# Sixteen sums of token pieces in the first layer: GpSimd in place of VectorE

## The chip, the cores and the metric

The kernel runs on one core of one Trainium2 chip. The metric is the device time of one execution in microseconds (us). The engines are TensorE (PE in the profile; PEld is its weight load), VectorE (DVE), ScalarE (ACT), GpSimd (POOL) and SyncE (SP), the last of which only issues DMAs here. Each engine works through its own queue in order; engines wait for one another by semaphores. GpSimd issues DMAs too, in the same queue as its own arithmetic.

## The reference, cut to what matters

Two layers, each on 512 tokens of 2048 features:

```
def hybrid_layer(x, ...):
    h = rmsnorm(x, g_pre)
    z = h @ w_in                 # the nine parts of z: two head groups and their gates
    ...                          # gated linear attention, chunked attention, SiLU gates
    y = jnp.concatenate([o_gla, o_att], axis=-1) @ w_out
    return x + rmsnorm(y, g_post)
```

All is float32. What matters here are the large products with `w_in` and the operand `h` that goes into them.

## The kernel before, in words

**Precision.** TensorE is fed in a rounded format (fp32r). Each operand is therefore split in two: a high part, which ScalarE makes by copying the value into the rounded format, and a low part, which VectorE makes by subtracting the high part from the value (`split`, lines 109 and 110, for tokens; `Job.high`, line 261, and `Job.low`, line 271, for weights). A product then is three matmuls: high by high, high by low, low by high.

**Products.** Most of the large products are done in pairs of blocks by the Strassen-Winograd scheme (`fast_gemm`): seven products P1 to P7, each over four chunks c of 512 features (two halves of 256), in place of eight. The token side is cut in four pieces: a11 and a12 from the first 256 tokens (feature halves 0 and 1, in `full[0, c][:, kh]`), a21 and a22 from the last 256 (`full[1, c][:, kh]`). P1, P2 and P4 take pieces as they are (a11, a12, a22). The others take sums of pieces: S1 = a21 - a22 for P5 (by the code's names), S2 = S1 - a11 for P6, S4 = a12 + S2 for P3, S3 = a11 - a21 for P7. With four chunks these are the sixteen sums of the title. They are made in place in the tiles of the pieces (128x512 float32) by `token_sums`: `make` picks the operands, `sub` does the sum, and `put` splits the result (high part on ScalarE, low part on VectorE) and stores the split in device memory for later block pairs by a DMA from GpSimd's queue.

**The weight side.** The raw weights come in by SP's DMAs, and VectorE makes the weight sums (lines 255 and 257). For the first pair of value blocks and for the pair of gate blocks ("parted" and "summed" in `Job`) the sum for P5 is made by the DMA itself: `Job.add` (lines 181 and 184) issues from GpSimd's queue a DMA that accumulates the second block onto the tile that held P1's weights. It has to wait until P1's high and low parts were read from that tile, and P5's high part waits until it has landed.

**The twin pairs of the first layer.** After the first gate block (`std_gemm`, lines 380 and following) the layer does the value pair (AV0, AV1: 512 columns) and the gate pair (AG1 with AG2: 264 columns) as twins: for each (k, c) of `PROD_TWIN` one step of the one and one step of the other, in the order P2, P1, P5, then P6 and P3 in turn, P7, P4. This takes about 50 to 168 us of the profile. In the same time `first_operands` (lines 783 and 799) still makes the pieces of the last 256 tokens, splits a22 and stores the split, and then `token_sums(0)` runs as a task: the first four sums (S1 of the four chunks) one after the other, and each later one only when the gate product that uses the sum of four places before has been written into the program, since the splits of S2, S4 and S3 share a ring of four buffers ("sa") with one another and with the splits of a22. The splits of S1 have homes of their own (`HOMES0`).

**What sets the order.** The program is laid out by a planner. It takes instructions by their place in the program and by when its own simulated clock has their data ready, for each engine. `tc.issue_after(x)` ties the instructions in its block that are on x's engine behind x on that engine; it says nothing to other engines. Before the change `sub` is tied on VectorE behind the low part made two jobs back (`lows[-2]`), and the high part in `put` behind the last weight cast on ScalarE (`last_cast[0]`). The second layer makes its sums elsewhere in its order and without such a tie.

The lines of the profile that matter: L473 matmuls of a fast product, L261 high part and L271 low part of a weight, L255 and L257 weight sums, L109 and L110 high and low part of tokens, L649 the token sums of both layers, L662 the store of a split token sum, L799 the store of the split a22, L181 and L184 the accumulating loads, L524 a small power on GpSimd in the norms of later parts.

Of the kernel before, what the change touches and what calls it, by code (L numbers as in the profile page):

```python
# [36 lines left out]
def hybrid_trunk(  # L37
# [14 lines left out]
    nc = tc.nc  # L52
# [20 lines left out]
    def slot(tag, shape, dtype=F32):  # L73
        return slots.tile([P] + shape, dtype, tag=tag, name=nm(tag))

    def rtile(tag, shape=(2, W), dtype=F32, bufs=4):
        return ring.tile([P] + list(shape), dtype, tag=tag, name=nm(tag), bufs=bufs)
# [27 lines left out]
    def flat(t):  # L105
        return t.bitcast(F32).rearrange("p a b -> p (a b)")

    def split(hi, lo, src):
        nc.scalar.copy(hi, src)  # L109
        return nc.vector.tensor_tensor(out=lo, in0=src, in1=hi.bitcast(F32), op=ALU.subtract).ins  # L110
# [39 lines left out]
    lows, loads, last_turn, first_high = [], [], [None], []  # L150
# [491 lines left out]

    def token_sums(l):
        tags, dst, home = ("g10", "g16", "H", "g0", "g1"), sa_d[l], HOMES if l else HOMES0
        stage, tied = [0], [False]

        def sub(out, a, b, op=ALU.subtract):
            with tc.issue_after(lows[-2]) if tied[0] else nullcontext():
                nc.vector.tensor_tensor(out=out, in0=a, in1=b, op=op)  # L649

        def put(name, c, src):
            if (name, c) in home:
                op = A[name, c] = slot(home[name, c], [2, 512], F32R)
            elif l == 0:
                op = A[name, c] = rtile("sa", (2, 512), F32R)
            else:
                tag = tags[stage[0] % len(tags)]
                op = rtile(tag, dtype=F32R) if tag == "H" else slot(tag, [2, 512], F32R)
                stage[0] += 1
            with tc.issue_after(last_cast[0]):  # L660
                split(op[:, 0, :], op[:, 1, :], src)
            nc.gpsimd.dma_start(dst[name, c], flat(op))  # L662
            written.add((id(dst), name, c))

        def make(name, c):
            a11, a12 = (full[0, c][:, kh, :] for kh in range(2))
            a21, a22 = (full[1, c][:, kh, :] for kh in range(2))
            if name == "S1":
                sub(a22, a21, a22)
                put(name, c, a22)  # L670
            elif name == "S2":
                sub(a22, a22, a11)
                put(name, c, a22)
            elif name == "S4":
                sub(a12, a12, a22, ALU.add)
                put(name, c, a12)
            else:
                sub(a21, a11, a21)
                put(name, c, a21)

        if l:
            for c in range(4):
                for name in ("S1", "S3", "S2", "S4"):
                    yield
                    make(name, c)
            yield
        else:
            names = [("S1", c) for c in range(4)] + [(n, c) for c in range(4) for n in ("S2", "S4")]
            names += [("S3", c) for c in range(4)]
            left = {v: k for k, v in LEFT.items()}  # L690
            for i, (name, c) in enumerate(names):
                tied[0] = True
                if i >= 4:
                    n, c0 = names[i - 4]
                    while (0, AG1, left[n], c0) not in issued:
                        yield
                make(name, c)
                yield
# [146 lines left out]
    def layer(l):  # L845
# [132 lines left out]
        if l:  # L978
            std_gemm(l, AG0, (0, 1), CO, operand_in, gate_evac(0), rate=1.3)
            roles.reverse()  # L980
            acc = {n: [ps_mm.tile([P, W], F32, tag="mm", name=nm("mm")) for _ in range(2)] for n in "YX"}
            fast_gemm(l, PAIRS[0], av_consume, rate=2.5, prod=PROD_FRONT, acc=acc)
            until(lambda: all((kh, 1, c) in A for kh in range(2) for c in range(4)))
            tasks.append(token_sums(l))
            std_gemm(l, AG0, (2, 3), CO, operand_in, gate_evac(0), rate=1.3)
            fast_gemm(l, PAIRS[0], av_consume, rate=1, prod=PROD_REST, acc=acc)
            drain()
            fast_gemm(l, GATE_PAIR, gate_consume, prod=PROD_GATE)
        else:
            std_gemm(l, AG0, range(NT), CO, operand_raw, raw_evac, rate=0.5, lag=1)  # L990
            acc = {n: [ps_mm.tile([P, W], F32, tag="mm", name=nm("mm")) for _ in range(2)] for n in "YX"}
            acc_g = {n: [aux()[:, :N1] for _ in range(2)] for n in "YX"}
            twins = [
                fast_gemm(l, pair, consume, rate=1, acc=z, steps=True)
                for pair, consume, z in ((PAIRS[0], av_consume, acc), (GATE_PAIR, gate_consume, acc_g))
            ]
            tasks.append(token_sums(l))
            for k, c in PROD_TWIN:
                if (k, c) == ("P5", 0):
                    acc["Z"] = [ps_mm.tile([P, W], F32, tag="mm", name=nm("mm")) for _ in range(2)]  # L1000
                for step in twins:
                    step(k, c)
            drain()
            roles.reverse()
# [664 lines left out]
```

## Time and profile before

| | |
|---|---|
| median of three runs | 1583.02 us (1580.74 to 1584.38) |
| the profiled execution | 1582.65 us, span of the instructions 1580.5 us |
| granted TensorE clock, mean | 0.999 |
| busy | PE 99%, DVE 81%, ACT 59%, POOL 9% of the span |
| token sums on VectorE (L649), both layers | 32 of about 0.68 us each |

How to read it. A busy time is a sum over the whole span; an engine that is busy 81% on the average can be full in one stretch and idle in another, so the stretch that the change touches has to be read by itself. A matmul's duration in the records overlaps the next one's, so the pace of TensorE is read from starts, not from durations. In a row of the timeline the first number is the start in us from the span's start, the second the duration, and a bracket at its end names how long the engine was idle before and what released it. In the chain of waits each row is a piece of the chain that ended last: start, length, and the engine and line that it went through.

### The profile page before, as it was taken

To read this page: it belongs to the slowest core of one execution; us is meant where nothing else is said; L and a number is where in the kernel's file an instruction comes from. 1 tells how busy PE (TensorE), PEld (TensorE's weight loads), DVE (VectorE), ACT (ScalarE), POOL (GpSimd) and SP (SyncE) were. 2 spreads that over 40 slices of the span, in tenths; PEclk is the share of its full clock that TensorE was granted. 3 is DMA by queue.
4 is the path that set the end of the run, shared out by engine and by line. 5 is a ranking of instruction groups with operands and counts; after the bars stand their busy time and mean duration, and the time that the engine had idled before them with its cause. 6 is when DMAs were issued, how large, how long until landed. Compare 5 with 4: busy or idle time off the path is not lost.

```text
span 1580.5 us, 24991 instructions
## 1 busy us (share of the span) xinstructions
PE 1570.5 (99%) x9054; PEld 1363.2 (86%) x9054; DVE 1287.6 (81%) x1723; ACT 928.6 (59%) x1551; POOL 138.9 (9%) x230
## 2 busy tenths in 40 slices
PE   9999999999999999999999999999999999999998
PEld 7888999998888777888888899999988887788886
DVE  5989968578786978998989878785886878699887
ACT  7655545657555556665786446455674655576644
POOL 0221000001000000100122000001010000001001
PEclk9999999999999999999999999999999999999999
DMA  9888895785859768689879998847969597686987
GB/s 370 264 263 295 306 332 190 229 304 183 312 173 313 271 227 306 241 301 387 304 250 360 368 332 312 307 148 235 332 213 313 175 334 263 233 297 226 343 302 206
DMA packets 137738, 439.40 MB, mean 278 GB/s; under 512 B 15364, under 2 KB 27908, under 8 KB 137584
## 3 DMA queue, kind: packets, MB, share of 16 engines
q1 hardware_dynamic: 118800, 372.65, 67.3%
q0 software_dynamic: 18528, 64.88, 12.1%
q8 instruction: 71, 1.16, 0.3%
q14 instruction: 51, 0.42, 0.1%
q10 hardware_dynamic: 288, 0.30, 0.1%
HBM read 378.20 MB, written 61.62 MB: 278 GB/s over the span
## 4 chain that ended last, share of the span: by engine, by line
PE 94%; DMA 3%; DVE 1%; ACT 1%; issue 0%; POOL 0%; SPq 0%; POOLq 0%; DVEq 0%; ACTq 0%
PE mm L473 54%; PE mm L463 20%; PE ax L473 6%; PE mm L380 4%; PE ax L1089 2%; PE ax L1071 1%; PE ax L1278 1%; PE ax L1248 1%; DMA g<-in_w_ag_dram 1%; DMA A<-sa 1%; PE ax L1051 1%; PE ax L1049 1%; PE ax L1050 1%; DVE wl L271 1%; DMA sa<-S 0%
## 5 line engine op out<-in xcount | busy, mean ns | idle before, releaser
L473 PE MATMUL mm<-wh,sa 128*128 128x512 f32 (+1 forms) x1600 | 502.6, 387 | 0.8 <-DMA sa<-S 0.8
L473 PEld LDWEIGHTS mm<-wh,sa 128*128 128x128 f32 x1600 | 296.9, 188 | 61.6 <-DMA sa<-S 1.2
L261 ACT CAST wh<-raw 128x1024 fp32r<-128x1024 f32 (+2 forms) x233 | 234.3, 1009 | 191.3 <-PE mm L473 69.5
L271 DVE TENSOR_TENSOR wl<-raw,wh 128x1024 fp32r<-128x1024 f32 (+2 forms) x233 | 269.5, 1162 | 75.9 <-PE mm L473 33.7
L261 ACT CAST wh<-H 128x1024 fp32r<-128x1024 f32 (+1 forms) x208 | 211.9, 1021 | 177.9 <-PE mm L473 62.3
L473 PE MATMUL mm<-wl,sa 128*128 128x512 f32 (+1 forms) x800 | 310.1, 388 | 0.4 <-DVE wl L271 0.4
L271 DVE TENSOR_TENSOR wl<-H,wh 128x1024 fp32r<-128x1024 f32 (+1 forms) x208 | 245.0, 1179 | 47.4 <-PE mm L473 18.3
L463 PE MATMUL mm<-sa,wh 128*128 128x256 f32 x1280 | 236.1, 284 | 0.0
L473 PE MATMUL mm<-wh,a 128*128 128x512 f32 (+1 forms) x672 | 215.4, 387 | 0.0
L463 PEld LDWEIGHTS mm<-sa,wh 128*128 128x128 f32 x1280 | 199.8, 191 | 0.5
L463 PE MATMUL mm<-sa,wl 128*128 128x256 f32 x640 | 180.6, 284 | 0.0
L473 PEld LDWEIGHTS mm<-wl,sa 128*128 128x128 f32 x800 | 150.2, 188 | 30.9 <-DVE wl L271 1.6
L473 PEld LDWEIGHTS mm<-wh,a 128*128 128x128 f32 x672 | 124.4, 188 | 24.2
L255 DVE TENSOR_TENSOR H<-H,raw 128x1024 f32<-128x1024 f32 (+1 forms) x120 | 141.0, 1180 | 0.3
L473 PE MATMUL mm<-wl,a 128*128 128x512 f32 (+1 forms) x336 | 130.8, 390 | 0.5 <-DVE wl L271 0.5
L261 ACT CAST wh<-g 128x1024 fp32r<-128x1024 f32 x84 | 81.3, 974 | 76.3 <-DVE g L255 25.7
L463 PEld LDWEIGHTS mm<-sa,wl 128*128 128x128 f32 x640 | 122.1, 191 | 0.2
L473 PE MATMUL mm<-wh,g 128*128 128x512 f32 (+1 forms) x416 | 120.5, 367 | 0.0
L271 DVE TENSOR_TENSOR wl<-g,wh 128x1024 fp32r<-128x1024 f32 x84 | 93.7, 1119 | 16.3 <-PE mm L463 7.4
L463 PE MATMUL mm<-a,wh 128*128 128x256 f32 x512 | 94.9, 285 | 0.0
L524 POOL TENSOR_TENSOR sm<-sm,mhalf 128x2 f32<-128x2 f32 (+2 forms) x40 | 38.9, 973 | 615.7 <-DVE sm L1099 295.7
L421 ACT COPY ev<-mm 128x512 f32<-128x512 f32 (+1 forms) x112 | 64.2, 573 | 45.8 <-PE mm L473 31.2
(284 smaller groups left out, 2493.7 us busy)
## 6 DMA issues: line engine op xcount, KB each, us to landing
raw<-in_w_dram SPq DMA_DIRECT2D x287, 512.0 KB, 5.4
sa<-S SPq DMA_DIRECT2D x176, 512.0 KB, 4.4
sa<-A SPq DMA_DIRECT2D x48, 512.0 KB, 6.0
H<-in_w_dram SPq DMA_DIRECT2D x48, 512.0 KB, 5.1
sa<-oS SPq DMA_DIRECT2D x32, 512.0 KB, 5.8
g<-in_w_dram SPq DMA_DIRECT2D x20, 512.0 KB, 7.0
S<-g POOLq DMA_DIRECT2D x18, 512.0 KB, 7.9
raw<-in_w_ag_dram SPq DMA_DIRECT2D x32, 264.0 KB, 4.5
```

Of the source, the lines that this page charges most:

```text
L255: nc.vector.tensor_tensor(out=h, in0=h, in1=r, op=ALU.add)
L261: last_cast[0] = nc.scalar.copy(self.wh[:, z, :], src[:, z, :]).ins
L271: last_low[0] = nc.vector.tensor_tensor(out=self.wl[:, z, :], in0=self.src[:, z, :], in1=self.wh[:, z, :].bitcast(F32), op=ALU.subtract).ins
L380: nc.tensor.matmul(pss[o], a(part, kk, o) if callable(a) else a[:, part, t], rhs[:, kk, :], start=(i == 0 and kk == 0 and m == 0), stop=(i ...
L421: last_copy[0] = nc.scalar.copy(e, src[t]).ins
L463: nc.tensor.matmul(dst, lhs[:, kk, f], a[:, part, tok], start=(fresh and kk == 0 and m == 0 and ft % 2 == 0), stop=(c == 3 and kk == 1 and ...
L473: last_mm[0] = nc.tensor.matmul(out_ps[t], a[:, part, tok], rhs[:, kk, :], start=(fresh and kk == 0 and m == 0), stop=(c == 3 and kk == 1 ...
L524: nc.gpsimd.tensor_tensor(out=out_r, in0=v, in1=mhalf[:, : v.shape[-1]], op=ALU.pow)
L1049: nc.tensor.matmul(ps[:, :n], self.qh[:, t], self.kh[:, :n], start=True, stop=False)
L1050: nc.tensor.matmul(ps[:, :n], self.qh[:, t], self.kl[:, :n], start=False, stop=False)
L1051: nc.tensor.matmul(ps[:, :n], self.ql[:, t], self.kh[:, :n], start=False, stop=True)
L1089: nc.tensor.matmul(o, self.pt[i][:, j * P : (j + 1) * P], av[hd // 4, j // 2][:, j % 2, (hd % 4) * P : (hd % 4 + 1) * P], start=(j == 0), ...
```

## The change

In the first layer the sixteen sums are issued on GpSimd in place of VectorE, and the tie behind the low part two jobs back goes. The operands, the results and the place in the program are the same, and so are `put` with its tie on ScalarE, the low parts on VectorE and the stores. The second layer's sums stay on VectorE; they had no tie before either, since `tied[0]` was set in the first layer's branch alone.

```
     def token_sums(l):
         tags, dst, home = ("g10", "g16", "H", "g0", "g1"), sa_d[l], HOMES if l else HOMES0
-        stage, tied = [0], [False]
+        stage = [0]
 
         def sub(out, a, b, op=ALU.subtract):
-            with tc.issue_after(lows[-2]) if tied[0] else nullcontext():
-                nc.vector.tensor_tensor(out=out, in0=a, in1=b, op=op)
+            (nc.vector if l else nc.gpsimd).tensor_tensor(out=out, in0=a, in1=b, op=op)
...
             for i, (name, c) in enumerate(names):
-                tied[0] = True
                 if i >= 4:
                     n, c0 = names[i - 4]
                     while (0, AG1, left[n], c0) not in issued:
```

More of the change, by code (lines that the diff above doesn't have):

```diff
@@ L644, in token_sums @@
         tags, dst, home = ("g10", "g16", "H", "g0", "g1"), sa_d[l], HOMES if l else HOMES0
-        stage, tied = [0], [False]
+        stage = [0]
         def sub(out, a, b, op=ALU.subtract):
-            with tc.issue_after(lows[-2]) if tied[0] else nullcontext():
-                nc.vector.tensor_tensor(out=out, in0=a, in1=b, op=op)
+            (nc.vector if l else nc.gpsimd).tensor_tensor(out=out, in0=a, in1=b, op=op)
         def put(name, c, src):
@@ L691, in token_sums @@
             for i, (name, c) in enumerate(names):
-                tied[0] = True
                 if i >= 4:
```

## The prediction, made before the result was known

> **What bounds the kernel now.** I read the page first, then the waits of TensorE over the whole span, then the stretch that holds the first layer's twin pairs (about 50 to 168 us) by windows, chain of waits and timeline.
>
> ```profile
> span 1580.5 us, 24991 instructions
> ...
> PE 1570.5 (99%) x9054; PEld 1363.2 (86%) x9054; DVE 1287.6 (81%) x1723; ACT 928.6 (59%) x1551; POOL 138.9 (9%) x230
> ...
> PE 94%; DMA 3%; DVE 1%; ACT 1%; issue 0%; POOL 0%; SPq 0%; POOLq 0%; DVEq 0%; ACTq 0%
> ```
> ```profile
> PE mm L473 <- DVE wl L271: 0.9, 2, 0.5
> PE mm L473 <- DMA sa<-S: 0.8, 1, 0.8
> ```
>
> TensorE (PE) is busy for 99% of the span and makes 94% of the chain that ended last. In the whole run its matmuls of the value and projection blocks waited 0.9 us for low parts from VectorE (DVE). So an edit that relieves DVE has little to win: it can only take away PE's waits, and those of the stretch in question are the next thing to price.
>
> The windows below are the stretch cut at its own turns: 66 to 82 holds the S1 sums, 82 to 101 the P5 pairs, 101 to 140 the P6/P3 and first P7 pairs. Columns: us, then busy time of PE, PEld, DVE, ACT, POOL, then clock, DMA share, GB/s.
>
> ```profile
> 66.00:82.00 16.00, 16.00 (x94) 14.18 (x93) 16.00 (x25) 10.98 (x18) 8.37 (x11) 1.00 1.02 250
> 82.00:101.00 19.00, 18.92 (x109) 16.56 (x108) 13.49 (x20) 8.28 (x13) 4.97 (x9) 1.00 0.99 302
> 101.00:140.00 39.00, 38.59 (x223) 33.81 (x222) 38.81 (x53) 24.49 (x39) 5.50 (x11) 1.00 0.70 237
> ```
>
> DVE has no idle time in 66 to 82, 5.51 us in 82 to 101 and 0.19 us in 101 to 140. PE lacks 0.08 and 0.41 us. DVE is full, but so is PE: a full DVE is here only just fast enough. Where PE did wait, its pace shows how much it lost:
>
> ```profile
> 96.96 0.39 PE L473 MATMUL mm<-wh,g 128*128 128x512 f32 x1
> ...
> 101.50 0.64 PE L473 MATMUL mm<-wh,sa 128*128 128x512 f32 x2
> ```
> ```profile
> 102.54 2.56 PE mm L473 x10
> 105.10 1.45 PE ax L473 x12
> 106.55 2.75 PE mm L473 x12
> 109.30 1.45 PE ax L473 x12
> 110.74 2.75 PE mm L473 x12
> ```
>
> A pair step (one value-block and one gate-block product) takes 110.74 - 106.55 = 4.19 us without a wait. The step from 96.96 to 101.50 took 4.54. The first P6 product, from 101.50, has its twelve value matmuls end at 105.10 by the chain, 3.60 after it began, where later ones have 2.75. The losses are so 0.35 and at most 0.85: the sums can win back at most about 1.2 us here. What made these losses is in the chain of the same stretch:
>
> ```profile
> 85.64 11.90 DMA g<-in_w_ag_dram
> 98.17 0.62 ACT sa L109
> 99.43 0.70 DVE wl L271
> 100.13 0.62 DVE g L255
> 100.75 0.60 DVE g L649
> 101.35 1.15 DVE wl L271
> ```
>
> The chain goes through GpSimd's (POOL's) DMA queue: the last accumulating load of a gate block (`add`, line 181), which lands at 97.54; then ScalarE's high part, and DVE's low part, a weight sum, one of the sixteen sums (L649, 0.60) and the low part that PE waits for.
>
> **The change part by part.** (1) Sixteen DVE sums go. One took:
>
> ```profile
> L649 DVE TENSOR_TENSOR g<-g x8: 674/680/693, 70.6 to 835.1; 128x512 f32<-128x512 f32 x8
> ```
>
> Back to back the next one starts 0.60 us later (100.75 + 0.60 = 101.35), so DVE is relieved of 16 x 0.60 = 9.6 us. Nearly all of it lies beside PE and is worth nothing; the one sum on the chain is worth 0.60.
>
> (2) Sixteen POOL subtractions or additions of 128x512 come. The trace has none; its nearest rows are fills:
>
> ```profile
> L753 POOL MEMSET t<- x1: 208/208/208, 13.4 to 13.4; 128x128 f32 x1
> L863 POOL MEMSET g<- x2: 277/277/277, 89.8 to 867.2; 128x192 f32 x2
> ```
>
> 64 columns more take 69 ns, so 512 columns are 277 + 320 x 1.08 = 623 ns for one pass. Two inputs and one output are one to three passes: 0.62 to 1.87 us. I take two passes, 1.24, since the write can run beside the reads. The Trainium skill (GPSIMD Engine Reference, "Elementwise — side-by-side cycle accounting") gives 4497 ns for 2048 columns; a quarter is an estimate of 1.12 us, and the sum would not move by it.
>
> (3) POOL's queue is in order, so each sum delays the DMAs behind it, and a sum waits behind a DMA that waits.
>
> ```profile
> 84.25 0.55 POOL L662 DMA_DIRECT2D S<-g  x1 [0.66 <-DMA A<-sa]
> 85.64 0.88 POOL L181 DMA_DIRECT2D g<-in_w_ag_dram  x1 [0.83 <-issue]
> ...
> 89.27 0.53 POOL L662 DMA_DIRECT2D S<-g  x1 [0.69 <-DMA S<-g]
> ```
>
> Here an issue waits for an earlier DMA to land ("<-DMA A<-sa", "<-DMA S<-g"): the queue is full, the add takes 11.90 us to land, and two issues are 1.39 us apart. So a late issue costs nothing while the queue has a backlog, and four sums (about 5 us) fit into the 7.63 us that POOL is not busy in 66 to 82. What costs is order: whatever is put ahead of the last add moves its landing by one place, about 1.3 us. The store of the fourth S1 (issued 89.27) can do so. Its sum waited on DVE until 81.50 although its input, the low part of A22, was done at 79.23:
>
> ```profile
> 78.55 0.68 DVE L110 TENSOR_TENSOR sa<-g,sa 128x512 fp32r<-128x512 f32 x1
> ...
> 81.50 0.68 DVE L649 TENSOR_TENSOR g<-g 128x512 f32<-128x512 f32 x1
> ```
>
> On POOL, without a tie, it can start at 79.3 and its split and store follow. Bounds 0 and +1.3 (+2.6, if a second store also goes ahead); I take +1.3, because that store was only 3.6 us behind the add.
>
> (4) The ties go. Instead of standing behind the low part two back, a sum can stand as soon as its data are there: the S3 sums after S1, S2 after the split of S1. So I expect many of the sums before 101, in the 5.51 us that DVE has idle, and the splits (their high parts still tied to the last cast on ScalarE) a little earlier. Nobody on DVE waits for them there.
>
> (5) Do POOL and DVE get in each other's way? This is the disputed cost. Rows of the small powers on POOL:
>
> ```profile
> 263.44 1.04 POOL L524 TENSOR_TENSOR sm<-sm,mhalf 128x4 f32<-128x4 f32 x1 [88.44 <-DVE sm L1099]
> ```
> ```profile
> 364.76 1.88 POOL L524 TENSOR_TENSOR sm<-sm,mhalf 128x4 f32<-128x4 f32 x1 [12.12 <-DVE sm L1099]
> ```
> ```profile
> 364.53 1.21 DVE L271 TENSOR_TENSOR wl<-H,wh 128x1024 fp32r<-128x1024 f32 x1
> ```
> ```profile
> 463.03 1.26 DVE L271 TENSOR_TENSOR wl<-H,wh 128x1024 fp32r<-128x1024 f32 x1
> ```
>
> The same power takes 1.04 us alone and 1.88 when DVE's two-input low part began 0.23 before it; it ended 0.90 after that low part (366.64 against 365.74). So POOL waited. The other way round the loss is small in the trace (a low part that began beside a power took 1.26 instead of 1.21), but that power reads four columns, not 512. Bounds for DVE's loss per sum: 0 and a whole POOL sum, 1.24 (1.87 at three passes). I take 0.6, about what DVE is relieved of, in the middle of 0 and 1.24: DVE is then neither freer nor fuller, and only the place counts. What a sum costs DVE in 66 to 82 delays PE by less than the roughly 1 us that PE would lose at 97 to 105 anyway while it waits for the last add; the two don't add.
>
> The sum: profiled execution 1582.65 (span 1580.5 and 2.15 around it); -0.60 for the sum that leaves the chain, +1.3 for the last add, 0 for DVE: 1583.35. The median of the three runs is 0.37 above the profiled one, so I forecast 1583.7 as a median. A measurement of this kernel can tell about 0.2%, 3.2 us: this is no change.
>
> **The rivals**, their times with the 0.37 as well. *A, relief only.* The store stays behind the add and POOL does not hold DVE up. Then all of 1.2 us comes back: 1581.8. For it: PE's waits there are DVE's low parts. Against it: the low parts waited for a DMA themselves. Still within 0.2%.
>
> *B, DVE becomes the bound (slower).* If a POOL sum keeps DVE from its two-input work for its whole length h, DVE's need grows. In the P6/P3 pairs:
>
> ```profile
> 104.23 1.22 DVE L271 TENSOR_TENSOR wl<-raw,wh 128x1024 fp32r<-128x1024 f32 x1
> ```
> ```profile
> 111.90 1.21 DVE L271 TENSOR_TENSOR wl<-raw,wh 128x1024 fp32r<-128x1024 f32 x1
> ```
>
> DVE turned two pairs round in 7.67 us with two sums among them, PE takes 2 x 4.19 = 8.38. With the sums on POOL DVE needs 7.67 - 1.20 + 2h, so it decides from h = 0.96. At h = 1.24 PE loses 0.57 in two pairs, at 1.5 1.09, at 1.87 1.83; the four such rounds (eight P6 and P3 pairs) make 2.3, 4.4 and 7.3 us. At 1.5: 1587.4, and 1590.3 at the end of it. For it: the power's 1.88, and DVE without idle time. Against it: sums that run before 101 aren't in these rounds, and then the rounds have 1.2 us to spare each. The Trainium skill (SBUF — State Buffer, "Who interferes with whom") says that a VectorE instruction with two inputs in SBUF and a GpSimd one that reads SBUF exclude each other, the second to issue waiting for the whole of the first; the trace agrees on POOL's side (1.88 against 1.04) and cannot show DVE's with 512 columns.
>
> *C, the queue.* Two stores and one POOL sum get ahead of the last adds while the queue runs dry: 2.6 + 1.2 - 0.6 = +3.2 at most, 1585 to 1586.2. For it: adds, stores and sums share one in-order queue; against it: the backlog.
>
> *D, something far away.* The planner lays out all later work anew, and waits of the other layers go (the 0.8 for sa<-S, the low parts). To be faster by 3.2 us nearly all of PE's waits would have to vanish: 1579.8.
>
> **How the numbers follow.** Forecast 0.47, A 0.17, B 0.24, C 0.08, D 0.04. The forecast's own range is 1582 to 1585.5. With A, C and the lower half of B, 1581.0 to 1587.5 holds a little over eight in ten. B counts as slower from 1586.2 (3.2 over the median), so from h = 1.4, which I hold for most of it, and with a little of C; D alone is faster: 0.04 faster, 0.72 no change, 0.24 slower.
>
> **What would show it.** Right: the sums stand on POOL at 1.0 to 1.9 us each, most before 101; DVE has more idle time in 82 to 101 or the same; the chain still goes over the last add, which lands at 98 to 99; PE's pairs keep 4.19. B: PE's matmuls wait for low parts several times in 66 to 140, low parts take over 1.5 us beside POOL sums. A: no wait at 97 to 105. Wrong altogether: a gain or loss outside 50 to 170 that is greater than inside.

## The result, and the profile after

| | before | after |
|---|---|---|
| median of six runs | 1582.08 us (1580.74 to 1584.38) | 1593.94 us (1592.46 to 1597.31) |
| profiled execution | 1582.65 us | 1593.94 us |
| granted TensorE clock, mean | 0.999 | 0.997 |

The changed kernel takes 1.0069 times as long (95% interval 1.0059 to 1.008): some 11 us slower, where the prediction said no change and a range up to 1587.5. It fell outside on the slow side.

The page of the changed kernel, for the lines shown of before: span, busy times, and the chain's shares by engine.

```profile
span 1591.4 us, 25003 instructions
...
PE 1575.6 (99%) x9054; PEld 1365.1 (86%) x9054; DVE 1298.9 (82%) x1707; ACT 928.4 (58%) x1551; POOL 168.8 (11%) x246
...
PE 95%; DMA 1%; DVE 1%; ACT 1%; issue 1%; POOL 1%; SPq 0%; POOLq 0%; DVEq 0%; ACTq 0%
```

VectorE has sixteen instructions fewer and is busy 11.3 us longer (1298.9 against 1287.6). That is the result in one line: what was taken off it came back, and as much again. The page alone doesn't say where; a share of 99% for PE looks the same in both.

The same three windows as before (us, then busy time of PE, PEld, DVE, ACT, POOL, clock, DMA share, GB/s):

```profile
66.00:82.00 16.00, 11.34 (x65) 9.30 (x64) 16.00 (x14) 8.98 (x16) 13.39 (x11) 0.96 0.97 226
82.00:101.00 19.00, 17.98 (x81) 14.74 (x82) 19.00 (x16) 5.62 (x9) 16.35 (x17) 0.85 0.90 231
101.00:140.00 39.00, 38.27 (x217) 33.17 (x216) 35.44 (x38) 22.27 (x35) 16.35 (x15) 1.00 0.61 214
```

Read the counts, not the busy times. In 66 to 82 VectorE was full before and is full now, but with 14 instructions instead of 25 (four of the 25 were sums); in 82 to 101 with 16 instead of 20, and its 5.51 idle us are gone. PE did 65 matmuls for 94 and 81 for 109. A full engine that does less work is being held up inside its instructions. The timeline of VectorE shows them:

```profile
77.53 4.17 DVE L271 TENSOR_TENSOR wl<-g,wh 128x1024 fp32r<-128x1024 f32 x1
...
82.84 2.44 DVE L110 TENSOR_TENSOR sa<-g,sa 128x512 fp32r<-128x512 f32 x1
...
88.66 3.18 DVE L110 TENSOR_TENSOR g<-g,g 128x512 fp32r<-128x512 f32 x1
91.76 1.21 DVE L271 TENSOR_TENSOR wl<-g,wh 128x1024 fp32r<-128x1024 f32 x1
...
93.50 3.23 DVE L271 TENSOR_TENSOR wl<-g,wh 128x528 fp32r<-128x528 f32 x1
```

A low part of 128x1024 takes 1.21 us (the row at 91.76); the one at 77.53 took 4.17. Beside it stand, on GpSimd's timeline (line 648 is the token sum in this kernel):

```profile
77.49 1.90 POOL L648 TENSOR_TENSOR g<-g 128x512 f32<-128x512 f32 x1
78.73 1.88 POOL L648 TENSOR_TENSOR g<-H,g 128x512 f32<-128x512 f32 x1
...
88.74 1.30 POOL L648 TENSOR_TENSOR g<-g,H 128x512 f32<-128x512 f32 x1
89.99 1.29 POOL L648 TENSOR_TENSOR g<-H,g 128x512 f32<-128x512 f32 x1
...
92.96 1.95 POOL L648 TENSOR_TENSOR g<-g,H 128x512 f32<-128x512 f32 x1
94.22 1.93 POOL L648 TENSOR_TENSOR H<-H,g 128x512 f32<-128x512 f32 x1
```

Two sums back to back (77.49 and 78.73) stand beside the 4.17 of VectorE's one row, two more (88.74, 89.99) inside the 3.18, where 0.68 is normal, and two more meet the 3.23 (0.70). Added up over 60 to 180 us, each VectorE row less the median of its form, 14 rows are together 20.7 us too long beside 16 sums: 1.29 us lost per sum, against 0.60 relieved. (One of the 14, at 76.03 and 1.09 too long, meets a sum's row in its last 0.11 only, and what held it is open; without it, 1.23 per sum.) A sum takes 1.29 to 1.31 where nothing holds it up. Of the sixteen, 12 start before 101 us and 15 before 107; the ties that spread them out are gone.

What PE saw (its timeline, the bracket names how long it was idle and for whom):

```profile
77.39 0.62 PE L473 MATMUL mm<-wh,a 128*128 128x512 f32 x2
81.75 0.80 PE L473 MATMUL mm<-wl,a 128*128 128x512 f32 x1 [3.74 <-DVE wl L271]
82.35 0.63 PE L473 MATMUL mm<-wh,a 128*128 128x512 f32 x1
82.77 0.63 PE L473 MATMUL mm<-wl,a 128*128 128x512 f32 x1
83.20 1.05 PE L473 MATMUL mm<-wh,a 128*128 128x512 f32 x2
```
```profile
83.00:85.00 2.00, 2.00 (x6) 1.52 (x6) 2.00 (x1) 0.00 (x0) 2.00 (x3) 0.50 1.00 186
87.00:90.00 3.00, 3.00 (x18) 2.69 (x17) 3.00 (x3) 1.11 (x2) 2.98 (x4) 0.91 1.03 270
```

PE waits 3.74 us for the 4.17 us low part. Of this wait 2.95 is what that row is too long; the rest had been lost ahead of it, where four rows from 66.59 to 76.03 are together 5.0 us too long. And then a second loss that no wait shows: matmuls start 0.43 apart (83.20 - 82.77) where the same kind starts 0.23 apart at full speed, and the windows (same columns) show the granted clock at 0.50 in 83 to 85 and at 0.91 in 87 to 90. In the trace's clock record it is halved from 80.7, 2.7 us into the wait, until 87.5. The Trainium skill (TensorE: Matmul & The Clock Gate, "Part 1: The HAM clock gate") says that an idle TensorE is cut to half its clock after a window of about 3.4 us and gets it back after as long a busy one. The trace agrees in kind, half clock from a wait of 3.74 and its return under work, but not on the length: in the experiments below waits of 2.21, 2.47 and 2.63 us were enough.

A way to see where time is lost without adding up waits: PE runs the same 9054 matmuls in all these kernels, in nearly the same order, so the n-th of one trace can be put beside the n-th of the other. The table gives how much later it starts than in the profile of before, for the matmuls that start there at the time on top; the last column but one is the loss inside the stretch (170 less 66). The rows of the experiments are read further below, under the same names.

| us later, at matmuls of before's | 66 | 82 | 105 | 142 | 170 | stretch | 1575 |
|---|---|---|---|---|---|---|---|
| after | -0.1 | 8.1 | 10.2 | 10.2 | 10.3 | 10.4 | 10.9 |
| vector_untied | 0.5 | 0.5 | 0.5 | 0.5 | 0.7 | 0.2 | 1.8 |
| gpsimd_tied | 0.1 | 0.4 | 1.1 | 7.6 | 8.1 | 8.0 | 10.5 |
| fill_beside | -0.1 | -0.1 | -0.7 | -0.7 | -0.8 | -0.6 | 1.7 |
| copy_beside | 0.0 | 0.0 | 0.2 | 5.8 | 6.2 | 6.2 | 7.0 |
| read_beside | 0.1 | 0.1 | 1.2 | 9.6 | 10.1 | 10.0 | 15.2 |
| s1_only | 0.0 | 4.1 | 3.1 | 3.1 | 3.0 | 3.0 | 5.3 |
| late_twelve | 0.5 | 6.0 | 9.4 | 9.4 | 9.2 | 8.7 | 9.8 |
| one_sum | -0.2 | -0.2 | -1.3 | -1.3 | -1.1 | -0.9 | 0.3 |
| fill_between | 0.2 | 0.5 | 0.6 | 4.6 | 6.9 | 6.7 | 7.9 |
| fill_untied | -0.4 | -0.4 | -0.3 | 4.0 | 3.8 | 4.2 | 5.9 |

The changed kernel loses nearly all of it between 66 and 105 and keeps nearly the same distance from there on. The last column moves by up to 5 us after the stretch in kernels whose sums are the same there (read_beside: from 10.1 to 15.2, fill_beside: from -0.8 to 1.7): so a profile's own span isn't enough for a difference of 2 us. Inside the stretch, too, fill_beside differs by 0.6 without one late row on VectorE, so that less than 1 us of one trace says little.

### The profile page after: what moved, and what is told of

Read it like the earlier page. It is cut to its first block, busy times and chain, and to the rows that moved or that the text cites. A ratio compares the mean times of both kernels' runs of the same rounds, so it can differ in the third digit from the quotient of the medians.

```text
span 1591.4 us, 25003 instructions
## 1 busy us (share of the span) xinstructions
PE 1575.6 (99%) x9054; PEld 1365.1 (86%) x9054; DVE 1298.9 (82%) x1707; ACT 928.4 (58%) x1551; POOL 168.8 (11%) x246
## 4 chain that ended last, share of the span: by engine, by line
PE 95%; DMA 1%; DVE 1%; ACT 1%; issue 1%; POOL 1%; SPq 0%; POOLq 0%; DVEq 0%; ACTq 0%
PE mm L473 55%; PE mm L463 20%; PE ax L473 6%; PE mm L380 4%; PE ax L1087 2%; PE ax L1069 1%; PE ax L1276 1%; PE ax L1246 1%; DVE wl L271 1%; PE ax L1049 1%; PE ax L1047 1%; PE ax L1048 1%; DMA sa<-S 0%; PE ax L1368 0%; PE ax L1112 0%
## 5 line engine op out<-in xcount | busy, mean ns | idle before, releaser
L271 DVE TENSOR_TENSOR wl<-g,wh 128x1024 fp32r<-128x1024 f32 x84 | 103.7, 1240 | 16.1 <-PE mm L463 7.1
```

The source lines that it names most:

```text
L271: last_low[0] = nc.vector.tensor_tensor(out=self.wl[:, z, :], in0=self.src[:, z, :], in1=self.wh[:, z, :].bitcast(F32), op=ALU.subtract).ins
```

## The experiments

Three theories were held against each other after the result. **Exclusion**: a GpSimd instruction that reads SBUF (the on-chip memory that holds the tiles) keeps VectorE's two-input instructions out, and each sum costs VectorE about its own length. **Queue**: sums in GpSimd's in-order queue delay the accumulating loads and stores (the last two loads were issued at 91.22 and 91.83 where before it was 80.51 and 85.64; the last landed at 98.20 against 97.54). **Ties**: the loss comes from sums moved early and bunched, whatever engine makes them. Ratios are against the kernel before on the same chip, with 95% intervals.

**The two parts of the change apart.** In vector_untied the sums stay on VectorE and only the tie goes:

```diff
-            with tc.issue_after(lows[-2]) if tied[0] else nullcontext():
-                nc.vector.tensor_tensor(out=out, in0=a, in1=b, op=op)
+            nc.vector.tensor_tensor(out=out, in0=a, in1=b, op=op)
```

> The sixteen sums stay on VectorE, only the tie goes. Exclusion theory (a GpSimd sum and VectorE's two-input work shut each other out for their whole length): no GpSimd sum, so no VectorE row longer than its usual 0.7 or 1.2 us; the sums come earlier but cost 0.6 each as before, so 1581 to 1585 us. Tie theory (the loss comes from the new order alone, whichever engine sums): most of the loss stays, 1589 to 1594 us. Queue theory (sums on GpSimd hold up the accumulating loads): 1581 to 1585 us.

Measured: 1584.19 us, ratio 1.0014 (1.0005 to 1.0024). No VectorE row is longer than normal, and the stretch loses 0.2 us. The rest of the ratio isn't in the stretch (the delay grows from 0.7 to 1.8 in later stages). Taking the ties away costs next to nothing where it acts, although the sums move early here too.

In gpsimd_tied they go to GpSimd, but tied there behind the store of the sum two places before (`stores` collects the store DMAs of `put`):

```diff
+            with tc.issue_after(stores[-2]) if len(stores) > 1 and not l else nullcontext():
+                (nc.vector if l else nc.gpsimd).tensor_tensor(out=out, in0=a, in1=b, op=op)
```

> The sums are on GpSimd, each behind the store of the sum two before it, so they come one by one over 65 to 140 us and not two back to back. Exclusion theory: each sum still shuts VectorE out for 1.2 to 1.4 us but VectorE gets in between; no row over 3 us, no long wait of TensorE, no fall of its clock; the P6 and P3 rounds lose about 0.7 us each: 1584 to 1588 us. Queue theory: the sums of S1 are still ahead of the accumulating loads, so P5 is as late as in the changed kernel: 1590 to 1594 us. Tie theory: 1581 to 1584 us.

Measured: 1593.72 us, 1.0068 (1.0053 to 1.0083). For the exclusion theory this was a miss by the number: spread out evenly, the sums should have cost less, and they cost the same. By the number alone the queue theory had it (1590 to 1594). But it put the loss at P5, and the table has 1.1 us lost by 105, where P5 is done, and the rest behind it; the last load landed at 95.94, earlier than before. The rows say where the loss is. VectorE, then GpSimd, of this kernel:

```profile
104.95 2.55 DVE L271 TENSOR_TENSOR wl<-raw,wh 128x1024 fp32r<-128x1024 f32 x1
...
109.78 2.33 DVE L255 TENSOR_TENSOR g<-g,raw 128x528 f32<-128x528 f32 x1
...
114.63 2.75 DVE L271 TENSOR_TENSOR wl<-raw,wh 128x1024 fp32r<-128x1024 f32 x1
```
```profile
104.50 0.57 POOL L662 DMA_DIRECT2D S<-sa  x1 [2.87 <-DVE sa L110]
105.10 1.31 POOL L649 TENSOR_TENSOR g<-g,H 128x512 f32<-128x512 f32 x1
...
110.23 1.30 POOL L649 TENSOR_TENSOR H<-H,g 128x512 f32<-128x512 f32 x1
...
114.99 1.31 POOL L649 TENSOR_TENSOR g<-g,H 128x512 f32<-128x512 f32 x1
```

Sums of 1.30 us cost VectorE 1.33 (2.55 - 1.22), 1.63 (2.33 - 0.70) and 1.53 us. The VectorE row of 104.95 began 0.15 *before* the sum's row and still waited for it to end, and so did that of 109.78, 0.45 ahead. One round of two pairs takes VectorE 114.63 - 104.95 = 9.68 us. Rival B of the prediction had written it as 7.67 - 1.20 + 2h; at the 1.5 lost here that is 9.5. PE's 8.38 is then too fast by 1.3, round after round; the clock stays at 1.00, and no wait is longer than 1.24:

```profile
PE mm L473 <- DVE wl L271: 5.9, 6, 1.2
```

The ties theory falls with these two kernels. Two different orders end at about the same loss (medians of 1593.94 and 1593.72 us; 10.4 and 8.0 us in the stretch), by two routes: a few long waits and a cut clock, nearly all before 101, or a small wait in each round at 103 to 148.

**Is it the instruction that reads, or GpSimd's being busy?** Three kernels keep VectorE's sums as they were before, ties too, and put extra work on GpSimd beside each, behind the store two places before. The extra work goes to a tile that nothing reads. (The first two of the sixteen wait for no store; they ran at 31 to 38 us, ahead of the stretch.)

```diff
             with tc.issue_after(lows[-2]) if tied[0] else nullcontext():
                 nc.vector.tensor_tensor(out=out, in0=a, in1=b, op=op)
+            if tied[0]:
+                with tc.issue_after(stores[-2]) if len(stores) > 1 else nullcontext():
+                    nc.gpsimd.memset(scr, 0.0)
+                    nc.gpsimd.memset(scr, 0.0)
```

This is fill_beside, two fills of 128x512 that read nothing. In copy_beside their place is taken by `nc.gpsimd.tensor_copy(scr, rb)`, one read of a constant tile, and in read_beside by `nc.gpsimd.tensor_tensor(out=scr, in0=rb, in1=rb, op=ALU.subtract)`, two.

> The kernel before, and beside each sum on VectorE two GpSimd fills of 128x512 (write only, together about 1.2 us) in the same places of its queue as the sums of the run before. It computes the same output. Exclusion theory with only reads shut out: VectorE rows keep their length, 1581 to 1584 us. Queue theory: GpSimd's queue is as full as with sums, 1586 to 1594 us. If writes shut VectorE out as well: VectorE rows of over 1.5 us and 1586 us or more.

> As the run with a GpSimd subtraction beside each sum of VectorE, but a GpSimd copy of 128x512 that reads one tile once. If any GpSimd read shuts out VectorE's two-input work for the length of the instruction, VectorE loses the copy's length, 0.6 to 0.9 us, sixteen times: 7.67 + 2 x 0.75 = 9.2 us per round, 1585 to 1590 us. If only a two-input GpSimd operation does: 1581 to 1584 us.

> As the fills, but beside each sum on VectorE one GpSimd subtraction of 128x512 that reads a constant tile twice and writes a scratch tile: nothing waits for its data, and VectorE keeps all its own work. Exclusion theory: VectorE loses 1.2 to 1.4 us per subtraction with nothing taken off it, 7.67 + 2.6 = 10.3 us per round of two pairs against 8.38: 1588 to 1596 us, worse than the run with the sums themselves tied on GpSimd. Queue theory: the same as with fills. Tie theory: 1581 to 1584 us.

Measured, in that order: 1582.52 us, 0.9997 (0.9988 to 1.0007); 1588.66 us, 1.0035 (1.0025 to 1.0046); 1594.23 us, 1.0074 (1.0053 to 1.0095). All three lie where the exclusion theory put them, the fills outside the queue theory's 1586 to 1594; that read_beside is worse than gpsimd_tied can't be told from 1594.23 against 1593.72. A VectorE sum and the GpSimd instructions beside it, one pair of fences for each kernel; the sum normally takes 0.68:

```profile
102.88 0.69 DVE L649 TENSOR_TENSOR H<-H,g 128x512 f32<-128x512 f32 x1
103.48 1.22 DVE L271 TENSOR_TENSOR wl<-raw,wh 128x1024 fp32r<-128x1024 f32 x1
```
```profile
103.16 0.55 POOL L652 MEMSET bias<- 128x512 f32 x1
103.77 0.53 POOL L653 MEMSET bias<- 128x512 f32 x1
```
```profile
113.61 1.46 DVE L649 TENSOR_TENSOR H<-H,g 128x512 f32<-128x512 f32 x1
```
```profile
113.89 0.62 POOL L652 COPY bias<-bias 128x512 f32<-128x512 f32 x1
```
```profile
104.79 1.96 DVE L649 TENSOR_TENSOR H<-H,g 128x512 f32<-128x512 f32 x1
```
```profile
105.14 1.05 POOL L652 TENSOR_TENSOR bias<-bias 128x512 f32<-128x512 f32 x1
```

Beside fills nothing moves. Beside this copy of 0.62 the sum loses 0.78, beside this subtraction of 1.05 it loses 1.28. Over 60 to 180 us all VectorE rows are 8.1 us too long beside 14 copies, 0.58 each, and 15.6 us beside 14 subtractions, 1.12 each. GpSimd's queue holds the extra instruction at about the same places in all three, so a queue made longer isn't the cause: 1.1 us of fills per sum are free, 1.05 us of reading cost as much as the whole change. The Trainium skill (SBUF — State Buffer, "Who interferes with whom") says the same of these kinds: a GpSimd instruction that only writes doesn't contend with a two-input VectorE one, one that reads excludes it for the whole instruction. The three runs agree in kind, and on the average in size: 0.58 lost for 0.62, 1.12 for 1.05.

**Which sums cost what.** In s1_only only the four S1 sums are on GpSimd, without a tie; the rest are tied on VectorE as before:

```diff
+            if tied[0] and which[0] < 4:
+                nc.gpsimd.tensor_tensor(out=out, in0=a, in1=b, op=op)
+                return
             with tc.issue_after(lows[-2]) if tied[0] else nullcontext():
```

In late_twelve the condition is `which[0] >= 4`: the twelve other sums (`which` counts them in the program's order).

> Only the four sums of S1 go to GpSimd, without ties; the other twelve stay on VectorE with theirs. Exclusion theory, with about 1.5 us of VectorE lost per sum (measured in the P6 and P3 rounds of the tied run, where a round took 9.8 us): four sums cost 6.0 and relieve 2.4, 3.6 us in the stretch 66 to 86 us where low parts are 1 to 3 us early, so TensorE loses 1 to 2.5 us: 1582 to 1585 us. Queue theory: these four are the ones that stand between the accumulating loads, so nearly all of the loss is here: 1590 us or more.

> Only the sums of S2, S4 and S3 go to GpSimd, without ties; S1 stays on VectorE with its ties. Exclusion theory: twelve sums cost 18 us of VectorE and relieve 7.2; they bunch from 75 to 110 us, where VectorE has 5.5 us idle and about 3 us of lead: 1587 to 1592 us. Queue theory: few of them stand before the accumulating loads: 1582 to 1585 us.

Measured: 1587.85 us, 1.0026 (1.001 to 1.0042), and 1592.02 us, 1.0052 (1.0037 to 1.0067). In the table the stretch loses 3.0 and 8.7, together 11.7 where the whole change loses 10.4: neither group is free. late_twelve is at the upper end of the exclusion theory's range (1592) and far above the queue theory's (1585). s1_only lies between the two, above the exclusion theory's 1585 and below the queue theory's 1590, in part because of the clock. PE's row after its wait, and the windows behind it:

```profile
78.84 0.50 PE L473 MATMUL mm<-wl,a 128*128 128x512 f32 x1 [2.21 <-DVE wl L271]
```
```profile
78.00:80.00 2.00, 1.16 (x5) 0.98 (x6) 2.00 (x4) 0.56 (x2) 0.91 (x2) 1.00 1.02 203
80.00:83.00 3.00, 3.00 (x12) 2.51 (x11) 3.00 (x4) 0.70 (x1) 2.92 (x5) 0.55 1.08 294
```

One wait of 2.21, and from 80.36, 1.5 us later, the matmuls start at half their pace. By their starts this costs 1.6 of the 3.0 us; the other 1.4 is inside the 1 to 2.5 that was expected of the stretch. The rest of the median's excess lies behind the stretch (5.3 at the end in this trace). In one_sum a single sum moves, S2 of the second chunk (`which[0] == 6`):

> Only the one sum that stood in the chain at 100.7 us (S2 of the second chunk) goes to GpSimd, without a tie; its data are ready some 15 us earlier. Exclusion theory: it costs VectorE 1.3 to 1.5 us near 80 us, beside lead, and takes 0.6 off the chain: 1581 to 1584 us, no change that can be measured. Relief theory (every sum taken off VectorE near the chain is a gain): 0.6 us faster, 1581.8 us.

Measured: 1583.34 us, 1.0001 (0.9992 to 1.001). In the stretch PE has no wait left at all, and the table shows a gain of 0.9 there, where the prediction had found 1.2 us to be won at most. That this is the relief is not shown: fill_beside has 0.6 of gain there with all its sums on VectorE. The median doesn't show it either. The one sum took 3.86 us at 77.51, while VectorE's rows beside it grew by 1.1 in all: here it was mostly GpSimd that waited. One sum at a place where VectorE has lead costs nothing that can be measured; sixteen do.

**What holds VectorE back before the sum's row begins?** In gpsimd_tied, most rows that began up to 0.45 us ahead of the sum lost too, but then the store's issue on GpSimd, just ahead of the sum, had already begun. If the sum claims its reads while that issue runs, a fill between the two should let such a VectorE row through. This is fill_between, which is gpsimd_tied with a fill of a tile that nothing reads, from the sixth sum on:

```diff
+            if len(stores) >= 5 and not l:
+                with tc.issue_after(stores[-1]):
+                    behind = nc.gpsimd.memset(scr[:, 0:192], 0.0).ins
+            with tc.issue_after(behind) if behind else nullcontext():
+                (nc.vector if l else nc.gpsimd).tensor_tensor(out=out, in0=a, in1=b, op=op)
```

> The tied GpSimd sums, and from the sixth sum on a GpSimd fill of 128x192 (0.28 us, write only) between the store that was just issued and the sum. In the tied run VectorE rows that began up to 0.36 us before the sum's own row were shut out too (2.23 us in place of 0.70), where the store's issue had begun before them. If the sum's claim on the reads begins during the issue ahead of it, the fill moves the claim later: VectorE loses 1.3 in place of 1.5 us per sum and a round of two pairs takes 9.4 in place of 9.8 us: 1590 to 1592 us. If the early rows only show how rows are recorded: the same length of rounds, 1592 to 1595 us.

Measured: 1590.55 us, 1.0038 (1.0025 to 1.0051). VectorE, then GpSimd:

```profile
117.94 0.70 DVE L255 TENSOR_TENSOR g<-g,raw 128x528 f32<-128x528 f32 x1
118.55 2.32 DVE L271 TENSOR_TENSOR wl<-g,wh 128x1024 fp32r<-128x1024 f32 x1
...
122.02 1.21 DVE L271 TENSOR_TENSOR wl<-raw,wh 128x1024 fp32r<-128x1024 f32 x1
```
```profile
118.27 0.28 POOL L651 MEMSET bias<- 128x192 f32 x1
118.49 1.30 POOL L653 TENSOR_TENSOR H<-H,g 128x512 f32<-128x512 f32 x1
...
122.57 1.82 POOL L653 TENSOR_TENSOR g<-g,H 128x512 f32<-128x512 f32 x1
```

The rows at 117.94 and 122.02 began 0.55 ahead of a sum and kept their length; at 122.57 the sum waited instead (1.82). A row that began 0.06 after the sum's start lost 1.10. Over 60 to 180 the loss per sum is 0.94 instead of 1.34. But this doesn't settle the early claim. Rows that began 0.50 and 0.59 ahead of a sum (124.42, 91.48) kept their length in gpsimd_tied too, without a fill, and so did three that began 0.14, 0.16 and 0.43 ahead (65.64, 70.63, 77.15). The fill moved the sum away from the row as well, and what decides who comes first stays open.

**Does the queue matter at all?** In fill_untied the sums are on VectorE without ties, and behind each stand, on GpSimd, a copy of one column of the result (so that it stands where a sum would) and two fills, all into a tile that nothing reads:

```diff
+            nc.vector.tensor_tensor(out=out, in0=a, in1=b, op=op)
+            if not l:
+                nc.gpsimd.tensor_copy(scr[:, 0:1], out[:, 0:1])
+                for _ in range(2):
+                    nc.gpsimd.memset(scr, 0.0)
```

> The sums stay on VectorE without ties, and behind each GpSimd copies one column of its result and does two fills of 128x512 (about 1.2 us, write only), without ties either, so that its queue is as full as in the changed kernel and the accumulating loads stand behind the fills. It computes the same output. Exclusion theory: as the run on VectorE without ties, 1582 to 1586 us, no VectorE row over 1.5 us. Queue theory (sums delay the loads, and so P5): 1588 to 1594 us.

Measured: 1587.8 us, 1.0027 (1.0016 to 1.0038): between what the two theories gave, and for a reason that neither had. GpSimd, then VectorE:

```profile
89.92 11.62 POOL L650 COPY bias<-g 128x1 f32<-128x1 f32 x1
```
```profile
100.25 1.24 DVE L271 TENSOR_TENSOR wl<-g,wh 128x1024 fp32r<-128x1024 f32 x1
101.76 0.71 DVE L271 TENSOR_TENSOR wl<-g,wh 128x528 fp32r<-128x528 f32 x1 [0.26 <-ACT wh L261]
```

A copy of one column takes 0.18 when undisturbed; this one took 11.62, and ended (101.54) in the first gap that VectorE left, 101.49 to 101.76. The accumulating loads weren't late (the last landed at 95.17; before, 97.54), but the stores of the sums behind the copy were, the next ones issued at 106.59 and 107.59. ScalarE's next high part waited until the second of them had landed:

```profile
113.84 0.62 ACT L109 CAST sa<-g 128x512 fp32r<-128x512 f32 x1 [6.25 <-DMA S<-sa]
```

VectorE then waited 5.91 us for that high part, and PE 2.47 us, up to 115.86, for a low part behind it. This wait and the half clock after it make nearly the whole loss of the stretch. So the queue can cost, but by starving, and that isn't what the changed kernel shows. In 60 to 125 us none of its instructions on PE, VectorE or ScalarE waits for a DMA, where before high parts waited 6.1 us for the accumulating loads; and nearly all of its loss is made before 105.

## Why the prediction was wrong

The step that failed is (5), and it failed in its size and in its last sentence.

*The size.* It put VectorE's loss per sum at 0.6, "in the middle of 0 and 1.24", so that what was lost equalled what was relieved and "only the place counts". Measured: 1.29 per sum in the changed kernel, 1.34 in gpsimd_tied, that is the upper bound and a little more. Sixteen sums cost VectorE 20.7 us and relieve it of 9.6. The bound was right and the middle of it was not a reasoned value: a row that met a sum mostly waited until the sum had ended, and the instruction kinds (two inputs on one side, 512 columns read on the other) were those for which that holds. The row that seemed to speak for a small loss, the low part of 1.26 beside a power, was of an operation that reads four columns.

*The last sentence*, that what a sum costs in 66 to 82 and the 1 us that PE lost at 97 to 105 "don't add". It took a late low part for something that a later wait absorbs. But PE was full in that stretch and VectorE without idle time, so nothing there absorbs anything: the delay is 8.1 us at 82 and doesn't shrink.

The other steps. (1) was not contradicted: one_sum has no PE wait left in the stretch and starts 0.9 us earlier behind it, but fill_beside comes to 0.6 without any relief, so the gain itself is not shown. (2) held: 1.24 taken, 1.29 to 1.31 measured undisturbed. (3) was the wrong thing to price. The last accumulating load landed at 98.20, inside the 98 to 99 that was forecast, but by luck: it was issued 6.2 us later than before and took 6.4 us in place of 11.9. And the +1.3 doesn't appear, because with VectorE and PE late nothing waits for that load any more:

```profile
DMA to landing us min/median/max: 4.0/6.3/7.4
```

This is the answer on the accumulating loads of line 181 in the changed kernel: they landed after 4.0 to 7.4 us, where they took 10.1 to 11.9 before. Why they were quicker was not tried. (4) was right in what it expected of the order, 12 of 16 sums before 101, and wrong that this was harmless ("Nobody on DVE waits for them there"): a sum on another engine isn't waited for, but it shuts VectorE out, and two in a row do so for 2.5 to 3 us in one go.

Of the rivals, B had the mechanism and its condition: h of 1.3 is past its 0.96, and its round is what gpsimd_tied shows. Its place was wrong for the changed kernel, and so its price: it counted the excess over PE's pace in the four P6/P3 rounds (1587.4 at h = 1.5) and dropped sums made before 101 as free. There the loss was larger, and the cut clock came on top (from 81.75 to 87.5 nine starts of 512 columns lose 0.20 each, the one behind the wait 0.26 and six narrow ones 0.10 each: 2.7 of the 10.4 us). What the clock adds was read from the starts and not tried alone. No kernel here beats the one before; one_sum equals it.

## What to carry to other kernels

Before work is moved from VectorE to GpSimd, look at what VectorE runs beside it: if those are instructions with two inputs and the moved one reads, price the move at the whole length of the GpSimd instruction added to VectorE, not at zero and not at half. It pays only where that is less than what VectorE is relieved of, or where VectorE has idle time for it. The average can come out lower where GpSimd is the one that waits (0.94 per sum in fill_between), but then a reason is needed why it would. And where an unknown cost has two ends because one engine either shuts the other out or doesn't, decide from the instructions which of the two it is; a middle taken for want of a reason is no estimate.

## What the runs showed of the hardware that was not expected

- An engine that is shut out doesn't always get in after the other's next instruction. The one-column copy stayed out for 11.62 us, and in the changed kernel a sum took 6.68, while VectorE went from 111.38 to 120.28 without a gap:

```profile
114.76 6.68 POOL L648 TENSOR_TENSOR H<-H,g 128x512 f32<-128x512 f32 x1
```

  In gpsimd_tied the sum at 124.92 came in between two VectorE rows that followed without a gap (it took 1.87, and the second row lost 1.10). What decides between the two is not known.
- Most VectorE rows that began up to 0.45 us before the row of a GpSimd sum behind a DMA issue lost its length, but three of gpsimd_tied didn't; why is open.
- One wait of 2.21 (s1_only) or 2.47 us (fill_untied) was enough for half clock behind it. It isn't always: in late_twelve a wait of 2.58 that ended at 83.80 had none behind it, one of 2.63 that ended at 91.94 had.
